# Differential attention's end on one Trainium2 core: the second output tile joins the stream

## The chip, the cores and the metric

One core of a Trainium2 chip. The time is device time in microseconds (us) of one execution, the median of three runs. A profiled execution of the same program supplies the rows. PE is TensorE's matmuls, PEld its weight loads, ACT ScalarE, DVE VectorE, POOL GpSimd, SP the engine that issues the DMAs here.

## The reference, cut to what matters

A two-layer encoder over 1024 tokens of width 1024, in float32. Layer 1 mixes tokens by dense differential attention with 8 heads, projects the result, and adds it normalised:

```python
h = rms_norm(x, g[0])
q, k, v = jnp.split(h @ w_qkv, 3, axis=-1)
s = jnp.einsum('bhmqd,bhmkd->bhmqk', qb, k) + bias      # two maps per head
a = jax.nn.softmax(s, axis=-1)
w = a[:, :, 0] - lam_full * a[:, :, 1]
o = jnp.einsum('bhqk,bhkd->bhqd', w, v)                 # then rms_norm per head
m = o.reshape(B, S, D) @ w_o                            # the output projection
x = x + rms_norm(m, g[1])
f = conv_glu_ffn(rms_norm(x, g[2]), ...)
...
x = x + gate * (p[i] @ ple_w_proj[i])
```

## The kernel before, in words

Matrix products with weights are made of three matmuls on split operands: a float32 is cut into a rounded high part (ACT, `high`) and a rest (DVE, `low`), and high x high, high x low and low x high are summed (`mm3`, `times_steps`). Tokens are worked in 8 tiles of 128.

Layer 1's attention (`da`) goes over 64 chunks, 8 heads times 8 token tiles. For chunk n, in PE's order: the value product of chunk n-1 (`da_values`, L642), the scores of chunk n+1 (`da_scores`, L606) into two PSUM tiles of pool "s", the two halves of the transposition of chunk n's weights (`da_turn`, L628), and the transposition of chunk n-1's normalised output (`da_out`, L656). Between them `tick` advances a generator, the stream (`qkv_stream`), by 6 steps a chunk. A step is a few matmuls of other work: first the projections to queries, keys and values, then the products of the embeddings (L1491 to L1494, stored to `pp`), last `first_out`: the output projection of token tile 0 over the first 7 of its 8 row blocks, 14 steps of alternately two and four matmuls into the two banks of pool "pj". The eighth row block is head 7's output, which the last eight chunks write into a page in SBUF (`opage`); rows 0 to 6 are read back from DRAM (`part_raw`, L787) and split (`part_of`).

Small works for ACT and DVE are a list of jobs. `job` takes one from the list twice per chunk and ties its instructions behind an instruction of that chunk on each of the two engines. `last_rows` puts there the splits of the projection's weight rows and of tile 0's part. `hurry` does the next job at once.

Then `mix_out` projects the tiles in the order 0, 4, 1, 5, 2, 3, 6, 7. For tile 0 only the eighth row block is left (6 matmuls); every other tile takes 48 (`product_of`). Behind each product go the squares (ACT, L918), their root (DVE L922, POOL L184), two multiplications and the residual sum (DVE, L928, L931), a second norm (ACT L179, DVE L180, POOL L184, DVE L192), which gives `h`. The transposition of tile n-1's `h` (L203) is issued behind the product of tile n; `put` splits it, with five sums more for tiles from 4 on.

PE's instructions run in the order in which the code issues them (`manual_schedule`). The order of the other engines is made by a planner with a model of durations, except where a region is ordered by hand: SP's first issues of `mix_out` (tile 4's load, two tiles of x, two gain vectors), and ACT and DVE from the last product on. Pools hand a page out again when its last reader is done.

Of the kernel before, what the change touches and what calls it, by code (L numbers as in the profile page):

```python
# [8 lines left out]
F32 = mybir.dt.float32  # L9
# [7 lines left out]
P = 128  # L17
D = 1024
SEQ = 1024
NT = SEQ // P  # L20
KT = D // P
# [5 lines left out]
D_HEADS = 8  # L27
FT = 22
PK = 2
EPS = 1e-6  # L30
LAMBDA_INIT = 0.8 - 0.6 * math.exp(-0.3)
RPITCH = 31
# [59 lines left out]
class Trunk:  # L92
# [27 lines left out]
    def page(self, pool, tag, shape=(P, D), dt=F32, **k):  # L120
        return pool.tile(list(shape), dt, tag=tag, name=self.uid(tag), **k)
# [54 lines left out]
    def rstd(self, src, junk, tag="ss"):  # L176

        ss = self.col(tag)
        self.nc.scalar.activation(junk, src, AF.Square, scale=D**-0.5, accum_out=ss)  # L179
        self.nc.vector.tensor_single_scalar(out=ss, in_=ss, scalar=EPS, op=ALU.add)  # L180
        return self.root(ss)
# [114 lines left out]
    def qkv_stream(self, layer, hT, x, first, mid):  # L296
# [98 lines left out]
        self.last_rows(layer)  # L395
        yield from emb
        yield from self.first_out()

    def begin(self, stream):
        self.stream, self.qk, self.v, self.credit = stream, {}, {}, 0.0  # L400
        self.jobs = []
# [233 lines left out]
    def da_values(self, x, n):  # L635
# [9 lines left out]
        nc.scalar.activation(os, o, AF.Square, scale=r0, accum_out=r)  # L645
        nc.vector.tensor_scalar(out=r, in0=r, scalar1=1.0 / P, scalar2=EPS, op0=ALU.mult, op1=ALU.add)  # L646
        self.root(r)
# [19 lines left out]
    def da(self, hT, oT, first, mid):  # L667

        N = NT * D_HEADS
        with self.tc.tile_pool(name="xa1", bufs=2, reuse_waits="tile") as x, \  # L670
             self.psum("s", 2) as self.ps:
            self.begin(self.qkv_stream(1, hT, x, first, mid))
            self.chunk = {}
            self.need(self.qk, 0)
            self.tick(6 / 6)
            self.da_scores(x, 0)
            self.tick(6 / 6)
            for n in range(N + 1):
                if n > 0:
                    self.need(self.v, (n - 1) // NT * 2 + 1)  # L680
                    self.da_values(x, n - 1)
                if n + 1 < N:
                    self.need(self.qk, (n + 1) // NT)
                    self.da_scores(x, n + 1)
                if n < N:
                    self.da_turn(x, n, 0)
                self.tick(0.34)
                if n < N:
                    self.da_turn(x, n, 1)
                self.tick(0.16)  # L690
                if n > 0:
                    self.da_out(x, n - 1, oT)
                self.tick(0.5)
            self.drain()

    def psum(self, name, bufs):
        return self.tc.tile_pool(name=self.uid("ps" + name), bufs=bufs, space=PSUM, reuse_waits="tile")
# [9 lines left out]
    def last_rows(self, layer):  # L707


        nc = self.nc  # L710
        src = self.i[("na_w_o", "da_w_o")[layer]]
        self.W, self.part0 = [], None
        page = lambda dt=F32R: self.page(self.r1, "r1", (P, 4, D), dt)
        pages = [page(), page(), page(F32)]
        raw = {}

        def load(kt):
            if kt < 4:
                raw[kt] = pages[2][:, kt]
            else:  # L720
                raw[kt] = self.page(self.raw, "raw")
            nc.sync.dma_start(raw[kt], src[kt * P : kt * P + P])

        def row(kt):
            if kt == 4:
                del pages[2]
                pages.extend([page(), page()])
            hi, lo = pages[2 * (kt // 4) : 2 * (kt // 4) + 2]
            parts = hi[:, kt % 4], lo[:, kt % 4]
            did = self.split(raw.pop(kt), *parts)  # L730
            self.W.append(parts)
            if kt == 4:
                raw["part"] = self.part_raw(layer, 0)
            if kt == 5:
                load(6)
            return did

        def part():
            self.part0 = self.part_of(raw.pop("part"))
            load(7)  # L740
            return self.did

        for kt in range(6):
            load(kt)
        self.jobs += [lambda kt=kt: row(kt) for kt in range(6)] + [part, None] + [lambda kt=kt: row(kt) for kt in (6, 7)]

    def job(self, act, dve):

        if self.jobs:
            todo = self.jobs.pop(0)  # L750
            if todo:
                self.behind(todo(), (act, dve))
# [45 lines left out]
    def first_out(self):  # L798
# [9 lines left out]
        self.row(KT - 1)  # L808
        self.out0 = hi, lo, m

    def mix_out(self, layer, x_in, x1):


# [4 lines left out]
        X = {k: self.page(self.r2, "r2", (P, 2, 4, 512), F32R) for k in ("B11", "T2", "B21", "T1")}  # L818
        self.xl = self.tc.tile_pool(name=f"xl{layer}", bufs=1, reuse_waits="tile", side="right")
        xl = self.xl.__enter__()  # L820
        with self.tc.tile_pool(name=f"xb{layer}", bufs=2, reuse_waits="tile") as x, self.psum("m", 2) as pm:
            W, last = self.W, self.opage
            order = (0, 4, 1, 5, 2, 3, 6, 7)
            b12, b21, b22 = (self.page(xl, k, (P, 4, 512)) for k in ("B12", "B21", "B22"))

            def load_x(t):
                xi = self.page(x, "x")
                nc.sync.dma_start(xi, self.rows_of(x_in, t, layer == 0))
                return xi
# [4 lines left out]
                return hi, lo, xi or load_x(t)  # L834

            with self.tc.manual_schedule(engines={ENG.SP}):
                second = self.out_part(layer, order[1])
                xs = [load_x(order[0])]
                g1 = self.bcast(x, "g1", self.i["norm_g"][layer, 1], bufs=1)
                xs.append(load_x(order[1]))  # L840
                g2 = self.bcast(x, "g2", self.i["norm_g"][layer, 2], bufs=1)
# [57 lines left out]
            def product_of(n, t):  # L899
                hi, lo, xi = ready.pop(0)  # L900
                part = [(hi[:, k], lo[:, k]) for k in range(KT)]
                h = hs[n] if n < 2 else self.page(x, "h")
                if n >= 2:
                    hs.append(h)
                if t == 0:
                    m = self.out0[2]
                    self.times(m, part[KT - 1 :], W[KT - 1 :], first=False)
                else:
                    m = pm.tile([P, D], F32, tag="m", name=self.uid("m"))
                    m = [m[:, :512], m[:, 512:]]  # L910
                    self.times(m, part, W)
                return m, h, xi
# [8 lines left out]
            def root_of(ss):  # L921
                nc.vector.tensor_scalar(out=ss[0], in0=ss[0], scalar1=ss[1], scalar2=EPS, op0=ALU.add, op1=ALU.add)  # L922
                return self.root(ss[0])
# [11 lines left out]
            for n, t in enumerate(order[:-1]):  # L935
                m, h, xi = product_of(n, t)
                residual(t, m, h, xi, root_of(squares(m, h)))
                self.normed(xi, h, g2)
                if n + 2 < NT:
                    ready.append(load(order[n + 2]))  # L940
                if n > 0:
                    self.transposed(hs[n - 1], put(order[n - 1], hs[n - 1]))
# [4 lines left out]
            self.region.__enter__()  # L947
            a, b = order[-2:]
            m, h, xi = product_of(NT - 1, b)
            (a1, a2), (b1, b2) = sums(hs[-2]), sums(h)  # L950
            ss = squares(m, h)
# [670 lines left out]
```

## Time and profile before

| what | value |
|---|---|
| median of three runs | 2741.68 us (2740.63 to 2742.09) |
| profiled execution | 2742.31 us, span 2740.5 us |
| mean granted clock of PE | 0.995 |
| PE busy | 2685.8 us (98%), 13440 matmuls |
| DVE, ACT, POOL busy | 1939.2, 1319.9, 463.8 us |
| 1890 to 1912 us: PE busy | 19.50 of 22.00 us |
| 1912 to 1925 us: PE busy | 13.00 of 13.00 us |
| 1925 to 1950 us: PE busy | 24.09 of 25.00 us |

The granted clock is a share of full speed: 1.00 is 2.4 GHz, 0.50 is 1.2 GHz. Ends of matmuls are modelled, so that consecutive ones overlap in the rows; the distance between starts, or between ends, is what PE spends on one. The last score product starts at 1895.4 us; the stretch of the change lies around 1890 to 1925 us.

### The profile page before, as it was taken

The page shows a single profiled execution, that of the slowest core. Times are in us where ns is not written, and L with a number is a line of the kernel's source. Part 1 is how long each engine was busy: PE and PEld are TensorE (multiplying, and loading weights), DVE is VectorE, ACT ScalarE, POOL GpSimd, SP SyncE. Part 2 cuts the span into 40 slices and gives each one's busy share as a digit, 9 for nine tenths or more (in the row PEclk, how much of TensorE's full clock was granted, in tenths as well). Part 3 has the DMA queues.
Part 4 walks back from the last instruction along what each step waited for, and adds up shares of the span by engine and source line. Part 5 has one row for each costly group of instructions (what it writes and reads, how often), then busy time and mean ns, then how long its engine had stood idle before and what let it go on. Part 6 is the DMA issues. An engine that isn't in the chain of part 4 may idle for free.

```text
span 2740.5 us, 36536 instructions
## 1 busy us (share of the span) xinstructions
PE 2685.8 (98%) x13440; PEld 2220.6 (81%) x13440; DVE 1939.2 (71%) x3317; ACT 1319.9 (48%) x2467; POOL 463.8 (17%) x461
## 2 busy tenths in 40 slices
PE   7999999999999999999999999999999999999998
PEld 6788888887888888888788888887877888888887
DVE  5677777689777787666466666666688777777664
ACT  4555556454434444454455555555454444444452
POOL 2121220104333400001000000000114333300000
PEclk9999999999999999999999999999999999999999
DMA  6412215523232273343211111123413333372343
GB/s 187 170 53 68 65 35 188 147 73 131 100 108 103 93 284 116 108 143 119 88 46 46 46 46 45 54 77 134 136 62 115 116 98 110 106 282 93 116 142 108
DMA packets 129475, 298.48 MB, mean 109 GB/s; under 512 B 11752, under 2 KB 37736, under 8 KB 129296
## 3 DMA queue, kind: packets, MB, share of 16 engines
q1 hardware_dynamic: 129296, 296.15, 32.9%
q8 instruction: 105, 1.72, 0.3%
q14 instruction: 74, 0.61, 0.1%
HBM read 221.69 MB, written 86.61 MB: 112 GB/s over the span
## 4 chain that ended last, share of the span: by engine, by line
PE 86%; DVE 6%; DMA 3%; ACT 2%; issue 2%; POOL 0%; SPq 0%; ACTq 0%; POOLq 0%; DVEq 0%
PE b L172 20%; PE b L173 20%; PE b L174 19%; PE g L778 6%; PE m L778 5%; PE b L642 4%; PE s L606 3%; PE b L628 2%; PE b L203 2%; PE av L512 1%; PE b L485 1%; DVE r L138 1%; DMA raw<-in_qkv 1%; PE b L778 1%; DMA x<-in_x 1%
## 5 line engine op out<-in xcount | busy, mean ns | idle before, releaser
L172 PE MATMUL b<-r,ws 128*128 128x512 f32 (+1 forms) x1328 | 548.1, 413 | 7.2 <-DVE u L1136 4.0
L173 PE MATMUL b<-r,ws 128*128 128x512 f32 (+1 forms) x1328 | 520.1, 392 | 1.1 <-DVE r L138 1.1
L174 PE MATMUL b<-r,ws 128*128 128x512 f32 (+1 forms) x1328 | 519.2, 391 | 0.5 <-DVE ws L138 0.5
L172 PEld LDWEIGHTS b<-r,ws 128*128 128x128 f32 x1328 | 252.8, 190 | 56.2 <-DVE u L1136 5.2
L174 PEld LDWEIGHTS b<-r,ws 128*128 128x128 f32 x1328 | 252.2, 190 | 55.0 <-DVE ws L138 1.0
L173 PEld LDWEIGHTS b<-r,ws 128*128 128x128 f32 x1328 | 253.5, 191 | 37.9 <-DVE r L138 2.9
L184 POOL TENSOR_TENSOR ss<-ss,mhalf 128x1 f32<-128x1 f32 x136 | 85.8, 632 | 1125.5 <-DVE ss L646 559.9
L172 PE MATMUL b<-r,wa 128*128 128x512 f32 x688 | 268.1, 390 | 4.0 <-DVE B L1148 3.7
L172 PE MATMUL b<-r,r 128*128 128x512 f32 x680 | 269.0, 396 | 1.6 <-ACT ws L1493 0.8
L445 ACT ACTIVATE E<-E,mn 128x1024 f32<-128x1024 f32 (+2 forms) x256 | 221.4, 866 | 101.7 <-DVE mn L441 101.4
L174 PE MATMUL b<-r,wa 128*128 128x512 f32 x688 | 268.0, 390 | 0.0
L173 PE MATMUL b<-r,wa 128*128 128x512 f32 x688 | 267.7, 389 | 0.0
L174 PE MATMUL b<-r,r 128*128 128x512 f32 x680 | 265.3, 390 | 1.0 <-DVE r L138 1.0
L173 PE MATMUL b<-r,r 128*128 128x512 f32 x680 | 265.4, 390 | 0.0
L138 DVE TENSOR_TENSOR ws<-raw,ws 128x512 fp32r<-128x512 f32 (+3 forms) x168 | 172.2, 1032 | 59.6 <-ACT ws L135 56.5
L138 DVE TENSOR_TENSOR r<-raw,r 128x512 fp32r<-128x512 f32 (+1 forms) x168 | 126.9, 762 | 106.7 <-ACT r L135 103.5
L135 ACT ACTIVATE r<-raw 128x512 fp32r<-128x512 f32 (+1 forms) x168 | 110.5, 665 | 187.7 <-PE b L173 162.6
L135 ACT ACTIVATE ws<-raw 128x512 fp32r<-128x512 f32 (+3 forms) x168 | 124.4, 748 | 133.0 <-PE b L174 52.4
L778 PE MATMUL m<-r,ws 128*128 128x512 f32 x672 | 156.0, 391 | 0.0
L778 PE MATMUL g<-r,ws 128*128 128x512 f32 x672 | 155.8, 391 | 0.0
L172 PEld LDWEIGHTS b<-r,wa 128*128 128x128 f32 x688 | 129.3, 188 | 32.4 <-DVE B L1148 5.0
L441 DVE CUSTOM_DVE_ANT_0 E<-s,T 128x1024 f32<-128x1024 f32 x128 | 151.1, 1218 | 3.6 <-PE s L606 3.6
(180 smaller groups left out, 5085.0 us busy)
## 6 DMA issues: line engine op xcount, KB each, us to landing
raw<-in_w_in SPq DMA_DIRECT2D x86, 512.0 KB, 3.5
raw<-in_qkv SPq DMA_DIRECT2D x48, 512.0 KB, 5.6
spillS<-r SPq DMA_DIRECT2D x88, 256.0 KB, 3.1
r<-in_ffn_w_out SPq DMA_DIRECT2D x40, 512.0 KB, 10.3
raw<-spillS SPq DMA_DIRECT2D x40, 512.0 KB, 3.5
spillA<-B SPq DMA_DIRECT2D x66, 256.0 KB, 3.0
raw<-spillA SPq DMA_DIRECT2D x30, 512.0 KB, 3.8
x<-x SPq DMA_DIRECT2D x24, 512.0 KB, 3.7
```

What stands on the lines that cost most here:

```text
L135: return self.nc.scalar.activation(hi, src, AF.Copy).ins
L138: return self.nc.vector.tensor_tensor(out=lo, in0=src, in1=hi.bitcast(F32), op=ALU.subtract).ins
L172: mm(out, sta[0], mov[0], start=first, stop=False, skip_group_check=onto)
L173: mm(out, sta[0], mov[1], start=False, stop=False, skip_group_check=onto)
L174: mm(out, sta[1], mov[0], start=False, stop=last, skip_group_check=onto)
L184: self.nc.gpsimd.tensor_tensor(out=ss, in0=ss, in1=self.mhalf, op=ALU.pow)
L203: self.nc.tensor.transpose(t[:, k * P : k * P + P], h[:, c : c + P], self.ident)
L441: nc.vector.tensor_tensor_reduce(out=e, in0=s, in1=bias, scale=1.0, scalar=3e38, op0=ALU.add, op1=ALU.min, accum_out=mn)
L445: self.exp = nc.scalar.activation(e, e, AF.Exp, bias=mn, scale=-1.0, accum_out=sm).ins
L606: nc.tensor.matmul(s[m][:, w], A[o, a, q], A[o, b, w], start=z == 0, stop=z == 2)
L642: nc.tensor.matmul(o, wT[:, k], V[:, k], start=k == 0, stop=k == KT - 1)
L778: mm(out[half], a, b[:, w], start=first and k + z == 0, stop=last and k == n - 1 and z == 2)
```

## The change

In layer 1, token tile 4's projection over its first 7 row blocks becomes the end of the stream (`second_out`), as tile 0's is already. Its load and split become the last job (`second`). Its PSUM tile comes from the scores' pool "s", which stays open through `mix_out` and supplies the later tiles too. At the last turn of the chunk loop (n = 64, no chunk left) the stream gets 0.6 of a chunk's steps before the last value product, and what is left of it is issued between that product and the last transposition. In `mix_out` tile 4 has 6 matmuls left. In layer 0 the PSUM pool has another name only.

```diff
@@ qkv_stream
         yield from self.first_out()
+        if layer == 1:
+            yield from self.second_out()
@@ da
-        with self.tc.tile_pool(name="xa1", bufs=2, reuse_waits="tile") as x, \
-             self.psum("s", 2) as self.ps:
+        self.spool = self.psum("s", 2)
+        self.ps = self.spool.__enter__()
+        with self.tc.tile_pool(name="xa1", bufs=2, reuse_waits="tile") as x:
...
             for n in range(N + 1):
+                if n == N:
+                    self.tick(0.6)
                 if n > 0:
                     self.need(self.v, (n - 1) // NT * 2 + 1)
                     self.da_values(x, n - 1)
                 if n + 1 < N:
                     self.need(self.qk, (n + 1) // NT)
                     self.da_scores(x, n + 1)
+                if n == N:
+                    self.drain()
                 if n < N:
                     self.da_turn(x, n, 0)
...
-            self.drain()
@@ last_rows
+        if layer == 1:
+            def second():
+                self.part1 = self.out_part(layer, SECOND)
+                return self.did
+
+            self.part1 = None
+            self.jobs += [None, second]
+    def second_out(self):
+
+        while self.part1 is None:
+            self.hurry()
+        hi, lo = self.part1
+        m = self.ps.tile([P, D], F32, tag="s", name=self.uid("m"))
+        m = [m[:, :512], m[:, 512:]]
+        yield from self.times_steps(m, [(hi[:, k], lo[:, k]) for k in range(KT - 1)], self.W, last=False)
+        self.out1 = hi, lo, m
@@ mix_out
-            order = (0, 4, 1, 5, 2, 3, 6, 7)
+            order = (0, SECOND, 1, 5, 2, 3, 6, 7)
...
-                second = self.out_part(layer, order[1])
+                second = self.out_part(layer, order[1]) if layer == 0 else self.out1[:2]
...
-                if t == 0:
-                    m = self.out0[2]
+                if t == 0 or layer == 1 and n == 1:
+                    m = (self.out1 if n else self.out0)[2]
                     self.times(m, part[KT - 1 :], W[KT - 1 :], first=False)
                 else:
-                    m = pm.tile([P, D], F32, tag="m", name=self.uid("m"))
+                    m = self.ps.tile([P, D], F32, tag="s", name=self.uid("m"))
```

## Rows read from the trace of the kernel before

**Rows 1.** The page's chain of waits, whole execution: shares of the span by engine.

```profile
PE 86%; DVE 6%; DMA 3%; ACT 2%; issue 2%; POOL 0%; SPq 0%; ACTq 0%; POOLq 0%; DVEq 0%
```

**Rows 2.** PE's waits, 1850 to 2050 us: us in total, times, longest.

```profile
PE b L656 <- DVE os L648: 1.9, 1, 1.9
PE b L203 <- ACT ws L135: 1.8, 2, 0.9
PE b L203 <- DVE h L968: 1.2, 1, 1.2
```

**Rows 3.** PE's instructions in time order: start, us, what, count, idle before and releaser.

```profile
1905.96 1.64 PE L778 MATMUL b<-r,ws 128*128 128x512 f32 x6
1907.43 1.95 PE L642 MATMUL b<-v,wT 128*128 128x128 f32 x16
1911.31 0.33 PE L656 MATMUL b<-ident,os 128*128 128x128 f32 x1 [1.93 <-DVE os L648]
1911.40 1.64 PE L778 MATMUL b<-r,ws 128*128 128x512 f32 x6
1912.87 11.07 PE L778 MATMUL m<-r,ws 128*128 128x512 f32 x48
1923.78 1.03 PE L203 MATMUL b<-ident,h 128*128 128x128 f32 x8
1924.57 11.15 PE L778 MATMUL m<-r,ws 128*128 128x512 f32 x48
```

**Rows 4.** All engines in time order, 1884.5 to 1890.7 us.

```profile
...
1887.47 0.95 ACT L135 ACTIVATE ws<-raw 128x896 fp32r<-128x896 f32 x1 [2.26 <-DMA pp<-ws]
...
1888.95 0.66 PE L628 MATMUL b<-ident,E 128*128 128x128 f32 x4 [0.73 <-ACT wT L631]
...
1889.93 0.58 ACT L1493 ACTIVATE ws<-b 128x512 f32<-128x512 f32 x1
...
1890.57 0.50 PE L778 MATMUL b<-r,ws 128*128 128x512 f32 x1 [0.61 <-ACT ws L1493]
```

**Rows 5.** All engines in time order, tile 0's chain, 1912.8 to 1924.5 us.

```profile
...
1912.62 1.15 ACT L135 ACTIVATE ws<-raw 128x896 fp32r<-128x896 f32 x2 [0.57 <-PE b L778]
...
1913.67 0.58 ACT L918 ACTIVATE h<-b 128x512 f32<-128x512 f32 x1
...
1915.31 0.55 POOL L184 TENSOR_TENSOR ss<-ss,mhalf 128x1 f32<-128x1 f32 x1 [4.50 <-DVE ss L922]
...
1917.34 1.23 DVE L931 TENSOR_TENSOR x<-h,x 128x1024 f32<-128x1024 f32 x1
...
1918.66 1.06 ACT L179 ACTIVATE h<-x 128x1024 f32<-128x1024 f32 x1 [3.74 <-DVE x L931]
...
1920.72 1.28 DVE L192 SCALAR_TENSOR_TENSOR h<-x,ss,g 128x1024 f32<-128x1024 f32 x1 [0.73 <-POOL ss L184]
...
```

**Rows 6.** All engines in time order, 1938.6 to 1939.2 us.

```profile
...
1938.73 0.68 DVE L874 TENSOR_TENSOR B<-B,B 128x512 f32<-128x512 f32 x1
1938.96 1.46 POOL L184 TENSOR_TENSOR ss<-ss,mhalf 128x1 f32<-128x1 f32 x1 [6.70 <-DVE ss L922]
```

**Rows 7.** All engines in time order, the end of tile 1's chain, 1935 to 1948.5 us.

```profile
...
1946.96 1.28 DVE L192 SCALAR_TENSOR_TENSOR h<-x,ss,g 128x1024 f32<-128x1024 f32 x1 [0.73 <-POOL ss L184]
...
1948.39 0.30 PE L203 MATMUL b<-ident,h 128*128 128x128 f32 x1 [0.91 <-ACT ws L135]
```

**Rows 8.** Busy us (instructions) of PE, PEld, DVE, ACT, POOL; granted clock; DMA share; GB/s.

```profile
2070.40:2072.60 2.20, 0.00 (x0) 0.00 (x0) 2.20 (x5) 0.00 (x0) 0.00 (x0) 1.00 0.88 292
...
2073.70:2077.00 3.30, 3.30 (x9) 2.62 (x8) 3.30 (x7) 2.84 (x4) 0.38 (x1) 0.50 0.57 195
...
1911.30:1915.00 3.70, 3.69 (x17) 3.05 (x18) 1.34 (x3) 2.67 (x7) 0.00 (x0) 1.00 0.58 236
```

**Rows 9.** PE's groups by shape, 16.6 to 22.2 us, then 22.5 to 26.4 us.

```profile
L172 PE MATMUL b<-r,ws 128*128 128x256 f32 x8 | 3.4, 424 | 0.0
...
L172 PE MATMUL b<-r,ws 128*128 128x256 f32 x8 | 2.3, 293 | 0.0
```

More of the change, by code (lines that the diff above doesn't have):

```diff
@@ L29 @@
 PK = 2
+SECOND = 4
 EPS = 1e-6
@@ L820, in mix_out @@
         xl = self.xl.__enter__()
-        with self.tc.tile_pool(name=f"xb{layer}", bufs=2, reuse_waits="tile") as x, self.psum("m", 2) as pm:
+        with ExitStack() as pools:
+            x = pools.enter_context(self.tc.tile_pool(name=f"xb{layer}", bufs=2, reuse_waits="tile"))
+            if layer == 0:
+                self.ps = pools.enter_context(self.psum("s", 2))
+            else:
+                pools.push(self.spool)
             W, last = self.W, self.opage
-            order = (0, 4, 1, 5, 2, 3, 6, 7)
+            order = (0, SECOND, 1, 5, 2, 3, 6, 7)
             b12, b21, b22 = (self.page(xl, k, (P, 4, 512)) for k in ("B12", "B21", "B22"))
```

## The prediction

> **What bounds the kernel now.** I read the chain of waits first: TensorE (PE) carries 86% of it [rows 1], so work taken off other engines earns nothing unless PE waits there. Then the list of PE's waits from 1850 to 2050 us, the stretch in which differential attention ends and its output projection runs [rows 2]: 1.9 us for the last chunk's normalised output (`os`), 1.8 us and 1.2 us for transposes of `h` further on. Then PE's instructions in order of time [rows 3]. The reader is to see there the order in which PE is fed, which is the order of the code, and that PE is full but for one hole: the last chunk's value product ends at 1909.38, its transposition starts at 1911.31, 1.93 us later. Behind it come six matmuls that finish output tile 0 (row block 7 alone, the stream did the rest), 48 for tile 4, eight transposes of tile 0's `h`, 48 for tile 1. The same view of all engines a little earlier shows a second, smaller loss [rows 4]: ScalarE (ACT), in order, sits in front of tile 4's 896-column split until a store of an embedding tile has landed (2.26 us), and PE waits 0.73 us and then 0.61 us for what stands behind that split.
>
> **The change part by part.**
>
> *Where the 42 matmuls go.* The stream now has 14 more steps of two or four matmuls. In the kernel before it runs dry in the last tick beside chunk 63: after 1905.96 six matmuls come where three steps would give eight [rows 3]. So second_out begins there with two, the new tick of 0.6 (3.6 credits, three steps) gives ten before the last value product, and the drain puts the other thirty between that product and the last transposition. The work is the same; 42 x 0.227 us = 9.5 us moves from behind that transposition to before it (0.227 us: 48 matmuls between the ends 1913.04 and 1923.94 [rows 3]).
>
> *The hole of 1.93 us.* Thirty matmuls are 6.8 us, more than the hole. Its whole length goes: -1.93 us. The scores' banks that the product takes were last read by chunk 63's softmax, long before; I cost that at nothing.
>
> *Tile 4's load and split.* They become the last job, called with chunk 63's scores and tied behind its exp on ACT and its last DVE sum. The load, one DMA, leaves SP's hand-ordered region, whose other four issues keep their order; it waits for a page of the raw pool as before and has until chunk 63 to land. The split's 0.95 us no longer stands before the transposed weights' copy of 1887.47 [rows 4], and by chunk 63 the stores it waited for have landed. Without it the embedding copy that PE waits for at 1890.57 still stands behind one exp, so I take 1.2 of the 0.73 + 0.61 = 1.34 us: -1.2 us, bounds 0 and -1.34. At its new place ACT and DVE have holes, and PE has first_out's matmuls to do.
>
> *What covered tile 0's chain.* This decides. In mix_out's loop PE's order is: tile 0's rest, tile 4's product, transposes of tile 0's `h`, tile 1's product. Before, tile 4's 48 matmuls (10.9 us) lay over the chain from tile 0's last matmul to its `h`: squares, root, residual, second norm [rows 5]. It ends at 1920.72 + 1.28 = 1922.00, that is 1922.00 - 1913.04 = 9.0 us after the last matmul, still 1.8 us ahead of PE. After, tile 4 has six matmuls there, 1.4 us. PE must then stand before the transposes for 9.0 - 1.4 = 7.6 us, and tile 1's 48 matmuls, whose operands are ready, are queued behind them.
>
> Tile 4's own chain now starts 1.4 us behind tile 0's instead of 11, and tile 5's split comes with it. By the durations of [rows 5] DVE has, between tile 0's residual sum and its `h`, room of 1.3 us and 0.7 us while ACT and POOL work; what it puts there (a split of 1.29 us, halves of 0.7 us) overruns by 0 to 0.9 us. I take 0.4: a wait of 8.0 us. Bounds: 7.0 us if the split that stands before the squares (squares start at 1913.67, 0.63 us after the matmul) moves away; 11.1 us if the chain is as long as tile 1's, which ran beside a loaded DVE from 1935.72 to 1948.24, 12.5 us [rows 3, 7].
>
> POOL's power instruction took 0.55 us in tile 0's chain [rows 5], but 1.46 us where DVE ran sums of two SBUF operands beside it [rows 6]. The Trainium skill, "SBUF — State Buffer", section "Who interferes with whom", says that such a DVE instruction and a GpSimd instruction hold one pair of ports by turns, each for its whole length; the trace agrees (0.91 us more), and by that rule alone tile 4's sums beside tile 0's power would make the wait 8.5 us, where undisturbed it is 7.6 us. My 8.0 us does not rest on it.
>
> *The clock after the wait.* PE stood idle from 2070.4 to 2072.6 (2.2 us). After that the granted clock was 0.50 (1.2 GHz) from 2073.7 to 2077.0, with PE busy all the time; after the hole of 1.93 us it stayed at 1.00 (2.4 GHz) [rows 8]. A wait of 8 us is far beyond the first. Half of 3.3 us is lost: 1.65 us. At the kernel's start, where PE had done next to nothing before, its stretch at the lower level is longer: 256-column matmuls show 424 ns to 22.2 us and 293 ns from 22.5 us [rows 9]; half of the 5.6 us is 2.8 us. The nearest row in kind is the first (PE was at full speed before), the nearest in length the second; I take 1.9 us, bounds 0 and 2.8.
>
> *Whether it is given back.* From tile 1 on the order on every engine is as before. PE's next waits there (0.91 us at 1948.39 [rows 7], its like for tile 2, 1.2 us at L968 [rows 2]) follow chains that begin with the end of a product by PE itself and so move along with it. I take nothing back; the bound is the sum of the two lines, -3.0 us. Layer 0 only renames its pool.
>
> *Sum:* -1.93 - 1.2 + 8.0 + 1.9 = +6.8 us. The profiled execution took 2742.31 us (span 2740.5 and 1.8 around it), 0.6 us above the median of 2741.68. On the median: 2748.5 us.
>
> **The rivals.**
>
> *A, slower by less.* The clock stays up, or the waits behind are shortened. For it: a hole of 1.93 us cost no clock [rows 8]; DVE is emptier beside tile 1's product, since tile 4's chain is done by then. Against: 2.2 us was enough, and DVE's load beside tile 5's product, where the chain of 12.5 us arises, is unchanged. Clock kept: -3.1 + 8.0 = +4.9, 2746.6 us. Clock lost but the 3.0 us repaid: +3.8, 2745.5 us.
>
> *B, slower by more.* DVE and ACT take tile 4's chain and tile 5's split ahead of tile 0's second norm, and the chain becomes as long as tile 1's: 11.1 us wait, -3.1 + 11.1 + 1.9 = +9.9 us; with the long clock spell +10.8, 2752.5 us. For it: that length occurs. Against: there DVE ran the five extra sums that `put` makes for a tile from 4 on, which nothing does beside tile 0's chain.
>
> *C, not slower.* PE does not stand at the transposes: tile 1's product passes them, or the order of the queue is not the one of the code. Place: PE's queue between tile 4's rest and tile 1; it decides whenever more than 1.4 us of the chain is left, and its worth is the whole 8.0 + 1.9. The time is then -3.1 us, 2738.5 us; with the later waits repaid as well -6.1, 2735.5 us. For it: tile 1's operands and banks are ready. Against: at 1911.31 PE waited 1.93 us with 54 matmuls queued whose operands were there [rows 3]. On this the Trainium skill, "TensorE: Matmul & The Clock Gate", section "Step-by-step: what each phase is for", says that weight loads may be pulled ahead, but matmuls stay in program order; by that C's gain is nothing and the wait stays, and the row agrees (none of the 54 passed).
>
> **How the numbers follow.** The forecast has 0.60, A 0.22, B 0.11, C 0.07. No change means within 0.2%, 5.5 us, about what a measurement of this kernel can tell. The forecast's own range is +5.2 to +8.3, some 0.04 of its 0.60 under +5.5; B is above. Slower: 0.56 + 0.11 = 0.67. Same: 0.04 + 0.22 + 0.03 (C's first form) = 0.29. Faster: C with all repaid, 0.04. The range goes from 2744.0 (A with both its gains in part) to 2752.0 us (B short of its end); it leaves out C, A's lower end and B's tail.
>
> **What would show it.** Right: 42 matmuls of `s` or `m` at L778 around the last value product; no wait before the last transposition; no split of 896 columns at the place of 1887.47; one PE wait of 7 to 9 us at L203 after twelve L778 matmuls; granted clock 0.50 for over 3 us from there; all later distances as before. Wrong: a wait there under 5 us, a clock of 1.00 behind it, or PE waits from tile 1 on that are shorter by more than 1 us.

## The result, and the profile after

The changed kernel takes 2747.9 us (median of 9 runs, 2746.72 to 2749.21), the kernel before in the same runs 2740.63 us: ratio 1.0027, 95% interval 1.0018 to 1.0035, 7.3 us slower. The profiled execution has a span of 2747.4 us against 2740.5, a mean granted clock of 0.993, and the same 13440 matmuls.

PE in order of time, changed kernel, where [rows 3] were (L645 is L642 before, L659 L656, L792 L778, L204 L203):

```profile
1904.11 1.64 PE L792 MATMUL b<-r,ws 128*128 128x512 f32 x6
1905.58 2.88 PE L792 MATMUL m<-r,ws 128*128 128x512 f32 x12
1908.30 1.95 PE L645 MATMUL b<-v,wT 128*128 128x128 f32 x16
1910.01 7.07 PE L792 MATMUL m<-r,ws 128*128 128x512 f32 x30
1916.91 0.27 PE L659 MATMUL b<-ident,os 128*128 128x128 f32 x1
1916.94 1.62 PE L792 MATMUL b<-r,ws 128*128 128x512 f32 x6
1918.40 1.52 PE L792 MATMUL m<-r,ws 128*128 128x512 f32 x6
1928.75 1.94 PE L204 MATMUL b<-ident,h 128*128 128x128 f32 x8 [8.84 <-DVE ss L951]
1930.35 12.45 PE L792 MATMUL m<-r,ws 128*128 128x512 f32 x48
1942.63 1.04 PE L204 MATMUL b<-ident,h 128*128 128x128 f32 x8
```

The 42 matmuls stand where they were counted to, 12 before the last value product and 30 behind it; the hole is gone; and before tile 0's transposes PE stands idle for 8.84 us, after which eight transposes take 1.94 us (1.03 before) and 48 matmuls 12.45 us (11.15). The releaser named is the instruction of DVE behind `h`, not `h` itself.

All engines in order of time there, changed kernel, tile 0's chain, where [rows 5] were:

```profile
...
1919.13 1.29 DVE L139 TENSOR_TENSOR ws<-raw,ws 128x896 fp32r<-128x896 f32 x2 [7.00 <-ACT ws L136]
1919.20 0.58 ACT L947 ACTIVATE h<-b 128x512 f32<-128x512 f32 x1
...
1920.84 0.55 POOL L185 TENSOR_TENSOR ss<-ss,mhalf 128x1 f32<-128x1 f32 x1 [9.15 <-DVE ss L951]
1921.42 1.41 DVE L957 SCALAR_TENSOR_TENSOR h<-b,ss,g 128x512 f32<-128x512 f32 x2 [0.73 <-POOL ss L185]
1922.75 1.28 DVE L139 TENSOR_TENSOR ws<-raw,ws 128x896 fp32r<-128x896 f32 x2
1923.95 1.22 DVE L960 TENSOR_TENSOR x<-h,x 128x1024 f32<-128x1024 f32 x1
...
1925.26 1.06 ACT L180 ACTIVATE h<-x 128x1024 f32<-128x1024 f32 x1 [3.78 <-DVE x L960]
...
1926.74 0.55 POOL L185 TENSOR_TENSOR ss<-ss,mhalf 128x1 f32<-128x1 f32 x1 [5.35 <-DVE ss L181]
...
1927.32 1.28 DVE L193 SCALAR_TENSOR_TENSOR h<-x,ss,g 128x1024 f32<-128x1024 f32 x1 [0.73 <-POOL ss L185]
...
```

From tile 0's last matmul (1918.56) to its `h` (1928.60) it is 10.0 us, 1.0 more than before: tile 5's split (L139 at 1922.75) now stands between the two multiplications and the residual sum.

Stretches of the changed kernel, columns as in [rows 8]: the wait, what follows it, and later. The clock has fallen within the wait and stays at 1.2 GHz for 4 us of work:

```profile
1919.90:1928.70 8.80, 0.02 (x1) 0.00 (x0) 6.01 (x11) 3.88 (x10) 1.10 (x2) 0.67 0.52 164
1928.70:1932.70 4.00, 3.95 (x14) 3.50 (x15) 3.27 (x6) 1.21 (x3) 0.55 (x1) 0.50 0.46 136
1933.20:1940.00 6.80, 6.80 (x32) 5.62 (x31) 1.44 (x2) 1.12 (x3) 0.55 (x1) 1.00 0.42 154
```

ACT in the changed kernel where [rows 4] had the split of 896 columns; the transposed weights' copy now comes as soon as PE has made them, and no embedding store is waited for:

```profile
1886.04 0.60 ACT L634 ACTIVATE wT<-b 128x512 f32<-128x512 f32 x1 [1.66 <-PE b L631]
1886.93 1.15 ACT L448 ACTIVATE E<-E,mn 128x1024 f32<-128x1024 f32 x1 [0.30 <-DVE mn L444]
```

Between the same instructions of PE in the two traces, with the moved work at 42 x 0.227 = 9.54 us:

| from, to | before | after | moved work in it | difference |
|---|---|---|---|---|
| value product of chunk 60, to that of chunk 61 | 9.56 | 8.57 | | -1.0 |
| to the end of first_out's 42 matmuls | 15.16 | 15.14 | | 0.0 |
| to tile 0's last matmul | 5.61 | 12.98 | +9.54 | -2.2 |
| to tile 0's transposes | 10.74 | 10.19 | -9.54 | +9.0 |
| to tile 4's transposes | 11.78 | 13.88 | | +2.1 |

The rows go from start to start, only tile 0's last matmul is taken by its end; first_out's 42 matmuls end where the next instruction starts. The sum is +7.9 us (+7.7 in the second executions below), while the spans differ by 6.9 us: the changed kernel's trace is 0.8 us earlier where the table begins (1881.87 against 1882.71) and 0.2 us shorter behind it. Neither can be put down to the change. The other kernels below that have the changed kernel's code ahead of that point reach it between 1881.63 and 1883.23 us; and from tile 4's transposes to the end of the span it is 804.9 and 804.3 us in two executions of the kernel before, 804.8 and 803.8 us in two of the changed one.

### The profile page after: what moved, and what is told of

It is laid out like the page before. It is cut to its first block, busy times and chain, and to the rows that moved or that the text cites. A ratio compares the mean times of both kernels' runs of the same rounds, so it can differ in the third digit from the quotient of the medians.

```text
span 2747.4 us, 36539 instructions
## 1 busy us (share of the span) xinstructions
PE 2689.0 (98%) x13440; PEld 2221.7 (81%) x13440; DVE 1940.6 (71%) x3317; ACT 1320.0 (48%) x2467; POOL 461.9 (17%) x461
## 4 chain that ended last, share of the span: by engine, by line
PE 86%; DVE 6%; DMA 4%; ACT 2%; issue 1%; POOL 0%; SPq 0%; ACTq 0%; DVEq 0%; POOLq 0%
PE b L173 19%; PE b L174 19%; PE b L175 19%; PE g L792 6%; PE m L792 5%; PE b L645 4%; PE s L609 3%; PE b L631 2%; PE b L204 2%; PE av L515 1%; PE b L488 1%; DVE r L139 1%; DMA raw<-in_qkv 1%; PE b L792 1%; DMA x<-in_x 1%
## 5 line engine op out<-in xcount | busy, mean ns | idle before, releaser
L139 DVE TENSOR_TENSOR ws<-raw,ws 128x512 fp32r<-128x512 f32 (+3 forms) x168 | 171.3, 1027 | 60.6 <-ACT ws L136 57.4
L139 DVE TENSOR_TENSOR r<-raw,r 128x512 fp32r<-128x512 f32 (+1 forms) x168 | 126.6, 760 | 106.8 <-ACT r L136 103.7
L792 PE MATMUL m<-r,ws 128*128 128x512 f32 x672 | 157.7, 393 | 0.0
L792 PE MATMUL g<-r,ws 128*128 128x512 f32 x672 | 155.8, 391 | 0.0
```

The lines of the kernel that those rows point to most:

```text
L139: return self.nc.vector.tensor_tensor(out=lo, in0=src, in1=hi.bitcast(F32), op=ALU.subtract).ins
L792: mm(out[half], a, b[:, w], start=first and k + z == 0, stop=last and k == n - 1 and z == 2)
```

## The experiments

**Work without use in the wait.** Does the slow stretch behind the wait come from the clock? 32 matmuls are put into the wait; their result is read by nobody.

```diff
                     self.times(m, part[KT - 1 :], W[KT - 1 :], first=False)
+                    if n == 1:
+                        idle = self.bank()
+                        for _ in range(32):
+                            nc.tensor.matmul(idle, W[0][0][:, :P], W[0][0][:, 512:], start=True, stop=True)
```

> The changed kernel with 32 matmuls more (7.3 us) into a PSUM bank that nobody reads, put on PE between tile 4's rest and tile 0's transposes. Theory: they lie wholly inside the wait of 8.8 us; about 1.5 us of it are left idle, the granted clock stays at 1.00, tile 0's transposes start at the same distance behind tile 0's last matmul (10.2 us), and the 2.1 us of half clock go: 2745.8 us. Rival (the slow stretch behind the wait is no matter of the clock but of DVE and ACT, which work beside it): the matmuls behind the wait stay slow and the time stays at 2747.9 us.

Measured: 2745.92 us, 1.0016 of the kernel before (1.0008 to 1.0025). PE in order of time:

```profile
1918.41 1.52 PE L792 MATMUL m<-r,ws 128*128 128x512 f32 x6
1919.77 7.42 PE L940 MATMUL b<-r 128*128 128x512 f32 x32
1928.77 1.07 PE L204 MATMUL b<-ident,h 128*128 128x128 f32 x8 [1.58 <-DVE ss L955]
```

and its stretch behind the wait, columns as before:

```profile
1928.70:1932.00 3.30, 3.23 (x19) 2.84 (x20) 2.57 (x6) 1.09 (x2) 0.55 (x1) 1.00 0.57 161
```

The transposes start 10.19 us behind tile 0's last matmul, as they did without these matmuls, and with the clock at 1.00 they take 1.07 us. From them to tile 4's transposes it is 11.82 us, as before the change (11.78), though DVE and ACT work beside it as in the changed kernel (13.88). So 2.1 us of the loss are the clock by the traces; by the medians it is 2.0 us, with intervals that overlap.

**Tile 5's split behind tile 0's `h`.** DVE's half of that split is tied behind the last instruction of tile 0's chain, for which `normed` and `split` hand out their instructions.

```diff
...
                 if n + 2 < NT:
                     ready.append(load(order[n + 2]))
+                    if layer == 1 and n == 1:
+                        self.behind(self.did + self.more, (first,))
```

> The changed kernel with DVE's half of tile 5's split tied behind tile 0's h. Theory (the chain grew from 9.0 to 10.0 us because that split of 1.28 us stands before tile 0's residual sum): the chain is 9.0 us again and PE's wait 7.7 us, the clock falls as before, 1.1 us gained, 2746.8 us. Rival (ACT's squares or POOL set the chain): wait 8.8 us and 2747.9 us.

Measured: 2747.9 us, 1.0022 (1.0013 to 1.0031). PE in order of time:

```profile
1918.15 1.52 PE L791 MATMUL m<-r,ws 128*128 128x512 f32 x6
1927.43 1.94 PE L203 MATMUL b<-ident,h 128*128 128x128 f32 x8 [7.76 <-DVE h L192]
1929.02 2.39 PE L791 MATMUL m<-r,ws 128*128 128x512 f32 x5
```

The wait is 7.76 us as expected, the chain 9.0 us again, and from the value product of chunk 60 to tile 0's transposes it is 45.80 us where the changed kernel has 46.88. The rival's wait of 8.8 us is refuted. The median did not show the 1.1 us: it is the rival's 2747.9, and the execution traced was the fastest of the ten (2746.2 us); the interval overlaps that of the changed kernel, so the time neither supports nor refutes the gain. What the trace shows is that the tenth microsecond of the chain was this split.

**Tile 1's product over tile 0's chain.** PE's order is changed in layer 1 only.

```diff
+                late = layer == 1 and n in (2, 3)
...
+                        c = {2: 7, 3: 4}[n]
+                        for _ in self.times_steps(m, part[:c], W[:c], last=False):
+                            pass
+                        self.transposed(hs[n - 2], put(order[n - 2], hs[n - 2]))
+                        h = self.page(x, "h")
+                        hs.append(h)
+                        self.times(m, part[c:], W[c:], first=False)
...
-                if n > 0:
+                if n > 2 or layer == 0 and n > 0:
                     self.transposed(hs[n - 1], put(order[n - 1], hs[n - 1]))
```

> The changed kernel, with the eight transposes of tile 0's h moved in PE's order behind 42 of tile 1's 48 matmuls, and those of tile 4's h behind 24 of tile 5's. Theory (the cost is PE's wait of 8.8 us before tile 0's transposes and the 2.1 us of half clock behind it; the rest of the change gains 3.2 us): no wait there, granted clock 1.00 all through, about 2737.5 us, 3 us under the kernel before; a new wait of up to 1 us where a tile's transposes now come sooner behind the last ones. Rival (the product in the scores' banks or the longer stream costs the time, and the wait only shows it): a wait of several us turns up elsewhere and the time stays at 2744 to 2748 us.

Measured: 2741.57 us, 0.9998 (0.9989 to 1.0007): 6 us less than the changed kernel, and 4 more than expected. The wait before tile 0's transposes is gone, but another came, before tile 1's. All engines in order of time there:

```profile
...
1944.35 0.69 DVE L139 TENSOR_TENSOR r<-h,r 128x512 fp32r<-128x512 f32 x1
1944.57 0.88 POOL L185 TENSOR_TENSOR ss<-ss,mhalf 128x1 f32<-128x1 f32 x1 [6.53 <-DVE ss L181]
...
1945.48 1.28 DVE L193 SCALAR_TENSOR_TENSOR h<-x,ss,g 128x1024 f32<-128x1024 f32 x1 [0.44 <-POOL ss L185]
...
1946.91 0.87 PE L204 MATMUL b<-ident,h 128*128 128x128 f32 x3 [2.85 <-DVE h L193]
```

Behind those 2.85 us the granted clock is 0.50 again, as the stretch there shows (columns as before):

```profile
1946.90:1948.40 1.50, 1.49 (x7) 1.50 (x8) 1.19 (x3) 0.36 (x1) 0.16 (x1) 0.50 0.43 71
```

Tile 4's transposes now stand in the middle of tile 5's product, and their sums run on DVE between the steps of tile 1's chain; the 24 matmuls behind them are over before that chain is. The rival's prediction of the time (2744 to 2748) fails as well; the wait of 8.8 us is the main cost, and covering it in one place uncovers another.

**All transposes later.** The same edit for five tiles, so that each has more of a product in front of it.

```diff
+                late = layer == 1 and 2 <= n < NT - 1
...
+                        c = {2: 7, 3: 4, 4: 4, 5: 4, 6: 2}[n]
...
-                if n > 0:
+                if n == NT - 2 or layer == 0 and n > 0:
                     self.transposed(hs[n - 1], put(order[n - 1], hs[n - 1]))
```

> The changed kernel with the transposes of tiles 0, 4, 1, 5 and 2 each moved into the product after the next, behind 42, 24, 24, 24 and 12 of its 48 matmuls. Theory (the wait of 2.85 us before tile 1's transposes, with the clock at half behind it, came because tile 4's sums and tile 1's chain stood in DVE's queue beside a product of which only half was left; with 5.4 us more in front of each of them nothing waits): no wait over 0.5 us between the last value product and the last tile, clock 1.00, 2737.4 us. Rival (DVE has more to do there than PE, so that any order only moves the wait): 2 to 3 us of waits stay, at later tiles, and 2740 to 2742 us.

Measured: 2735.63 us, 0.998 (0.9972 to 0.9989). One stretch from chunk 63 to the last tile, columns as before; PE is never idle in it and the clock never falls:

```profile
1905.00:1992.00 87.00, 87.00 (x420) 72.72 (x419) 52.19 (x81) 35.83 (x81) 9.01 (x15) 1.00 0.44 148
```

DVE has 52 us of work in 87: not the limit, only its order was. This version is faster than both kernels, 12 us under the changed one. The table's 9.0 and 2.1 us and the changed kernel's waits of 0.34 and 0.37 us before tile 1's and tile 2's transposes make 11.8 of them.

**Two row blocks instead of seven.** Only 12 of the 42 matmuls go to the stream, without the tick of 0.6.

```diff
-                if n == N:
-                    self.tick(0.6)
...
-        yield from self.times_steps(m, [(hi[:, k], lo[:, k]) for k in range(KT - 1)], self.W, last=False)
+        yield from self.times_steps(m, [(hi[:, k], lo[:, k]) for k in range(2)], self.W, last=False)
...
-                    self.times(m, part[KT - 1 :], W[KT - 1 :], first=False)
+                    done = 2 if n else KT - 1
+                    self.times(m, part[done:], W[done:], first=False)
```

> The changed kernel with only two of tile 4's seven row blocks in the stream (12 matmuls, 2 beside chunk 63 and 10 behind the last value product, without the tick of 0.6); 36 stay in mix_out. Theory: ten matmuls (2.3 us) still fill the hole of 1.93 us, 36 x 0.227 = 8.2 us cover a chain of 9.0 to 10.0 us, so a wait of 0.8 to 1.9 us is left, too short for the clock to fall: 1.0 + 2.1 gained, 0.8 to 1.9 lost, 2738.5 to 2739.5 us. Rival (banks or stream): the scores' banks are used as before, so 2744 us or more.

Measured: 2738.53 us, 0.999 (0.9981 to 0.9998). PE in order of time:

```profile
1906.05 0.62 PE L790 MATMUL m<-r,ws 128*128 128x512 f32 x2
1906.51 1.95 PE L645 MATMUL b<-v,wT 128*128 128x128 f32 x16
1908.21 2.53 PE L790 MATMUL m<-r,ws 128*128 128x512 f32 x10
1910.58 0.27 PE L659 MATMUL b<-ident,os 128*128 128x128 f32 x1
1910.60 1.63 PE L790 MATMUL b<-r,ws 128*128 128x512 f32 x6
1912.07 8.32 PE L790 MATMUL m<-r,ws 128*128 128x512 f32 x36
1921.35 1.06 PE L204 MATMUL b<-ident,h 128*128 128x128 f32 x8 [0.96 <-DVE h L193]
```

Ten matmuls fill the hole, 36 leave 0.96 us of the chain open, and the clock stays: the transposes take 1.06 us. The product sits in the same banks and in the same stream as in the changed kernel: a rival that blames these is refuted.

**Two row blocks, and six matmuls of tile 1 first.** Tile 0's transposes stand behind the first row block of tile 1's product.

```diff
...
+                        for _ in self.times_steps(m, part[:1], W[:1], last=False):
+                            pass
+                        self.transposed(hs[0], put(order[0], hs[0]))
...
+                        self.times(m, part[1:], W[1:], first=False)
```

> The kernel with two row blocks in the stream, with tile 0's transposes behind the first 6 of tile 1's 48 matmuls (1.4 us). Theory: they cover the 0.96 us that were left before those transposes, tile 0's chain of 9.2 us is then hidden whole, no wait above 0.4 us up to the last product, 2737.6 us. Rival (DVE is the limit there, each later transposition gives its wait to the next): the 1 us comes back at tile 1's transposes, 2738.5 us.

Measured: 2736.99 us, 0.9983 (0.9974 to 0.9992). PE in order of time, at tile 0's and at tile 1's transposes:

```profile
1922.49 1.03 PE L204 MATMUL b<-ident,h 128*128 128x128 f32 x8
...
1945.21 1.06 PE L204 MATMUL b<-ident,h 128*128 128x128 f32 x8 [0.37 <-DVE h L193]
```

Nothing waits at tile 0's transposes any more, 0.37 us at tile 1's and at tile 2's each, as with two row blocks alone. By time it can't be told from the kernel with all transposes later.

**The job alone.** The kernel before, with only tile 4's load and split moved to the last job.

```diff
...
+            self.part1 = None
+            self.jobs += [None, second]
...
-                second = self.out_part(layer, order[1])
+                second = self.out_part(layer, order[1]) if layer == 0 else self.part1
```

> The kernel before with one part of the change: tile 4's load and split become the last job, its product stays whole in mix_out behind the last transposition. Theory (ACT's wait for the store, ahead of the transposed weights' copy, cost PE about 1 us, and that gain is apart from all else): no 896-column split between 1885 and 1897 us, PE's wait of 0.73 us for the copy gone, the hole of 1.93 us and the later stretch as before, 1.0 us gained, 2740.3 us. Rival (the split costs the same wherever it stands): PE waits about 1 us near chunk 63 instead, 2741.3 us.

Measured: 2739.49 us, 0.9993 (0.9984 to 1.0002). PE's waits from 1880 to 2060 us (total, times, longest): the hole stands, and the wait for the weights' copy (`wT`, [rows 4]) is not in the list any more:

```profile
PE b L657 <- DVE os L649: 1.9, 1, 1.9
PE b L204 <- DVE h L976: 1.2, 1, 1.2
PE b L173 <- DVE B L1156: 1.0, 1, 1.0
PE b L204 <- DVE h L193: 0.7, 2, 0.4
PE b L786 <- ACT ws L1501: 0.5, 1, 0.5
...
```

The gain of 1 us is there in the trace (8.56 us from value product to value product, 1882.38 to 1890.94, 9.56 before); by time it is not clear of no change.

**Both kernels again.** Unchanged, one execution each.

> The kernel before, unchanged, for a second look. The changed kernel's trace shows 0.34 and 0.37 us before tile 1's and tile 2's transposes, where the kernel before showed 0.91 and 0.90. If that 1.1 us belongs to the change, this trace shows 0.9 us twice again; if it is the chance of one execution (POOL's power instruction, 1.46 or 0.86 us beside DVE's sums), one or both are 0.4 us here. The ACT wait of 2.26 us for the embedding store and the hole of 1.93 us should stand in it again.

> The changed kernel, unchanged, for a second look: the wait before tile 0's transposes 8.8 us again, the granted clock 0.50 for about 4 us behind it. If the 0.4 us before tile 1's and tile 2's transposes are chance, one of them can be 0.9 us here.

Measured: 2741.8 and 2747.94 us. PE's instructions that waited, kernel before, this second execution:

```profile
1889.14 0.65 PE L628 MATMUL b<-ident,E 128*128 128x128 f32 x4 [0.77 <-ACT wT L631]
...
1890.76 1.90 PE L778 MATMUL b<-r,ws 128*128 128x512 f32 x7 [0.62 <-ACT ws L1493]
...
1911.51 0.33 PE L656 MATMUL b<-ident,os 128*128 128x128 f32 x1 [1.94 <-DVE os L648]
...
1948.04 1.06 PE L203 MATMUL b<-ident,h 128*128 128x128 f32 x8 [0.37 <-DVE h L192]
...
1972.17 1.07 PE L203 MATMUL b<-ident,h 128*128 128x128 f32 x8 [0.37 <-DVE h L192]
```

The hole and ACT's two waits belong to the kernel; the 0.9 us that the first trace had before tile 1's and tile 2's transposes each do not, it is 0.37 us here. So the change gives nothing back there. The changed kernel showed 8.83 us at its wait again, and 13.70 us from tile 0's to tile 4's transposes (13.88 in the first execution; 11.79 in the kernel before).

## Why the prediction was right

Forecast +6.8 us, measured +7.3, by the mechanism that was forecast. Term by term:

- **The 42 matmuls**: 12 before the last value product and 30 behind it, as counted.
- **The hole**: forecast -1.93; -2.2 in the table. It is gone whole. The forecast took the hole from the value product's end, which is modelled; by starts, PE spent 3.88 us from that product to the transposition (1907.43 to 1911.31) where it spends 1.71 us when matmuls follow at once (1908.30 to 1910.01), so the hole was worth 2.17 us.
- **Tile 4's split**: forecast -1.2; -1.0 in the table, and the same with the job alone. Of PE's two waits the first went; of the second 0.55 us stayed.
- **The wait before tile 0's transposes**: forecast 8.0, measured 8.84. The part of 7.6 us was right to 0.2 (7.76 us with the split tied back). The addition to it was too small and at the wrong place: I let DVE take tile 5's split between the residual sum and `h`, where there is room; it took it ahead of the residual sum, and nearly the whole 1.28 us went into the chain.
- **The ports of DVE and POOL**: POOL's power instruction took 0.55 us both times in this chain. The 8.5 us worked out from the Trainium skill ("SBUF — State Buffer", "Who interferes with whom") lies nearer to 8.84 than my 8.0, but not for its reason.
- **The clock**: forecast 1.9; 2.1 in the table and by the trace with matmuls in the wait, 1.9 in the second executions.
- **Nothing is given back**: right. By its letter one sign of being wrong was there: two later waits are 1.1 us shorter than in the first trace of the kernel before (0.34 and 0.37 us for 0.91 and 0.90). But the kernel before has 0.37 us twice in its second execution, so this is not the change.
- **The sum**: the table's +7.9 us is 1.1 us over the forecast's +6.8, and nearly all of that is the wait, 9.0 us where 8.0 were taken. That the time of 2747.9 us came within 0.6 us of the forecast's 2748.5 is in part luck: the forecast added too small a rise to a median of three runs that was 1.05 us higher than that of the nine.

Rival A would have needed the clock or those later waits to turn; rival B a chain of 12.5 us, measured 10.0. Rival C is refuted: tile 1's 48 matmuls stood 8.84 us behind the transposes and none passed them, in agreement with the Trainium skill ("TensorE: Matmul & The Clock Gate", "Step-by-step: what each phase is for": matmuls go in program order). Put before them by hand, the same matmuls took the wait away.

## What to carry to other kernels

Work that is moved into a hole leaves a place, and what it covered there must be counted like the hole itself: here 9.5 us went into a hole of 1.9 us, and a chain of 9 us lost its cover. Move what the hole holds and no more (two row blocks were faster than before where seven were slower), or move the consumer of the chain back by as much. When one consumer is moved back, look at the next one on the same engine: moving the transposes of the first two tiles brought a wait of 2.85 us at the third's, moving those of five tiles none.

## What the hardware showed beside this

Two executions of the same program differ at the same place: POOL's power instruction beside DVE's sums of two SBUF operands took 1.46 us in one [rows 6] and 0.86 us in the other at the same instruction, and PE's wait behind that chain was 0.91 or 0.37 us. In both the power instruction ended 0.4 us after the end of one of these sums: of the second (L870, to 1940.02) in the first execution, of the first (L874, to 1939.59) in the other. Differences of half a microsecond between two single traces are therefore no evidence. And of PE's idle times, 0.96 us and 1.58 us left the granted clock at 1.00, while 2.85, 7.76 and 8.84 us were each followed by 0.50.
